# Delta rule outputs split where they are made, and a second merge that loads both operands directly

## The chip, the core and the metric

The kernel runs on one core of one Trainium2 chip. The metric is device time in microseconds (us) of one execution; runs are told by their median. The engines are named as in the profile: PE is TensorE's matmul side, PEld its weight loads, DVE is VectorE, ACT is ScalarE, POOL is GpSimd, and SP is the SyncE queue, which issues nearly all DMAs in order.

## What is computed

One inference step of a decoder layer for two groups of requests that share one set of weights: a prompt of 1024 tokens and a decode group of 8 sequences with 4 tokens each (32 columns). Model width is 1024. Cut to what matters here:

```
h = RMSNorm(x);  p = h @ w_in
  -> attention q|k|v (8 heads x 64), conv input of the delta rule, gate z, decays a, b, gate_A, gate_B
branch A: stick-breaking attention over 8 heads                      -> o_A (512 wide)
branch B: short conv, SiLU, gated delta rule, 4 heads, 128x128 state;
          o = RMSNorm(o) * gdn_norm_w * silu(z)                      -> o_B (4 heads x 128 = 512 wide)
merge:    m = sigmoid(gate_A) * (o_A @ w_pa) + sigmoid(gate_B) * (o_B @ w_pb);  x = x + m @ w_o
mixer:    x = x + relu(RMSNorm(x) @ w_up)^2 @ w_down;  final RMSNorm
```

The change is about o_B on its way from branch B into the product o_B @ w_pb, which is called the second merge here (its steps are named pb).

## The kernel before

Activations are held transposed: 128 features on the partitions, tokens along the row. T = 1056 columns are the 1024 prompt tokens and the 32 decode tokens. Every large product is made of three matmuls with operands split in two. The rounded part is the value in the type fp32r, written by an ACT copy; the rest is the value less the rounded part, written by a DVE subtraction. `dense` multiplies rounded weight by rounded activation, rounded weight by the activation's rest, and the weight's rest by the rounded activation (L137, L138, L139). `load_w` loads a block of weights and splits it in the same way (L127 on ACT, L128 on DVE).

The order of instructions on each engine is not written by hand. The program gives a sequence with priorities, and a planner at build time simulates it and sets the order of each engine's queue; `tc.high_priority()` moves steps ahead, `tc.issue_after` holds a step behind another. Tiles live in pools that are opened and closed like a stack, and a pool that is opened later takes over the space of closed ones. Tiles with one tag share one buffer (or as many as `bufs` says).

The steps in the order of the program, where the change touches them:

1. Four heads of the delta rule, `gdn_head(h)`. Their projections run interleaved with the chunk-wise recurrence (8 chunks of 128 tokens). In a head, `vb` (tag vb, one buffer) is the scaled v, read by the recurrence at L551; `qe` (tag cgb, one buffer) is loaded from cg_d at L489, goes through an exponential on ACT (L490) and a product on DVE (L491), and is read by the recurrence at L568. At the head's end the output is normalised, transposed on PE and multiplied by silu(z) into `zl` (L585). `zl` has the tag cgb too, so it takes qe's buffer, and the next head's qe takes its. L586 stores zl into `o_d[4 + h]` in DRAM.
2. The decode group's delta rule, in one go for all heads and sequences. Its output `dot` goes into the last 32 columns of `o_d[4:8]` (L778). The pools of this part and of the decode attention (`kts` and others) take over the space of the heads' pool.
3. The attention's projections and the prompt's attention, a pipeline over blocks (head, row block): scores on PE (L958, L959), sigmoid on ACT (L960), masking and 1 - s on POOL (L961, L964), a scan on DVE (`pr`, L968) and a product on DVE (L969), transposes on PE (`wt`, L111), and products with v (`po`, L1006). In `pipeline(x0, x1, fill)` other steps are put between the blocks: first the products of the gates (`pd_g`, whose outputs `gt` are stored to gA_d and gB_d, L1073), and from block 34 on the steps of the second merge, `pb_step(j, c, first)`, for 8 blocks of output columns and 4 groups of tokens c (256, 256, 256, 288 columns).
4. The operands of the second merge, `obh[c]` (rounded part) and `obl[c]` (rest), for the four groups of tokens. A group of o_B is loaded from o_d into a staging tile, `ofb0` to `ofb3` (L1111 for the first, L1153 for the others), copied into obh[c] on ACT (L1155), and subtracted into obl[c] on DVE (L1156). ofb0 lies in the pool zp and is loaded ahead of the close of the projections' pools; ofb1 and ofb3 share one buffer of the pool z2p; ofb2 lies in the pool obp beside obh and obl. Between the third and the fourth group two rows of gate B are loaded (`tbs`, L1159); the others are loaded by `pb_step` behind `mark`, the last operand load.
5. `pb_step` multiplies by w_pb with `dense4`, and DVE multiplies the result by gate B into tb (L1174).
6. Then the first merge (o_A @ w_pa, steps pa), w_o, and the mixer.

Of the kernel before, what the change touches and what calls it, by code (L numbers as in the profile page):

```python
# [8 lines left out]
F32 = mybir.dt.float32  # L9
F32R = mybir.dt.float32r  # L10
I32 = mybir.dt.int32
I64 = mybir.dt.int64
AF = mybir.ActivationFunctionType
ALU = mybir.AluOpType
# [4 lines left out]
P = 128  # L19
D = 1024  # L20
NP = 1024
NS = 32
T = NP + NS
# [8 lines left out]
GH = 4  # L32
# [6 lines left out]
def hybrid_step(ctx, tc, x_prompt, x_sample, cache_k, cache_v, page_table, state_conv, state_ssm,  # L39
# [5 lines left out]
    V, S_, G, PE, SY = nc.vector, nc.scalar, nc.gpsimd, nc.tensor, nc.sync  # L45
# [12 lines left out]
    dr = ctx.enter_context(tc.tile_pool(name="dr", bufs=1, space=DRAM))  # L58
# [30 lines left out]
    for t in range(9):  # L89
        xn = sp.tile([P, D], F32, tag="xn", name=f"xn{t}", bufs=7)  # L90
        n = P if t < 8 else NS
# [4 lines left out]
        if t in (1, 3, 5):  # L96
            wp = wpool if t == 1 else gw if t == 5 else sp
            st = wp.tile([P, 8, P], F32, tag="wst", name=f"ws_u0{t}", bufs=1)
# [47 lines left out]
    xT_d, o_d, x1_d = spill("xT_d"), spill("o_d"), spill("x1_d")  # L146
    gA_d, gB_d = spill("gA_d"), spill("gB_d")
    z_d = dr.tile([GH, P, NP], F32, name="z_d")
    q_d = [dr.tile([4, P, NP], F32, name=f"q{x}_d") for x in "hl"]
    k_d = [dr.tile([4, P, NP], F32, name=f"k{x}_d") for x in "hl"]  # L150
    v_d = dr.tile([4, P, NC, P], F32, name="v_d")
# [32 lines left out]
    zp = pool("zp", stack=zctx)  # L184
# [7 lines left out]
    for t in range(9):  # L192
        n = P if t < 8 else NS
# [65 lines left out]
    gk = pool("gk", stack=gctx, side="right")  # L259
# [129 lines left out]
    def gdn_head(h):  # L389
# [12 lines left out]
        for i, (src, tag) in enumerate(((kT, "ms"), (qT, "tv"))):  # L402
            sq = gk.tile([P, NP], F32, tag=tag, name=f"sq{i}{h}")
            S_.activation(sq, src, AF.Square)
            for hf in range(2):
                sqt = gk.tile([P, 512], F32, tag="x2", name=f"sqt{i}{h}{hf}")
                V.transpose(sqt, sq[:, hf * 512:(hf + 1) * 512])
                o = 32 * i + 16 * hf
# [35 lines left out]
        for c0 in range(0, NC, 2):  # L444
            pt = ttile(f"kk{h}_{c0}")
            for c in (c0, c0 + 1):
                sl = slice(c * P, (c + 1) * P)
                o = (c - c0) * 2 * P
                PE.matmul(pt[:, o:o + P], lhsT=kT[:, sl], rhs=kT[:, sl], start=True, stop=True)
                PE.matmul(pt[:, o + P:o + 2 * P], lhsT=kT[:, sl], rhs=qT[:, sl], start=True, stop=True)  # L450
            for c in (c0, c0 + 1):
                sl = slice(c * P, (c + 1) * P)
                o = (c - c0) * 2 * P
# [16 lines left out]
        for k in range(31):  # L470
            nr = 31 - k
            ob = gk.tile([32, 256], F32, tag="ob", name=f"ob{h}_{k}")
# [11 lines left out]
        vb = gk.tile([P, NP], F32, tag="vb", name=f"vb{h}")  # L484
# [50 lines left out]
        for hf in range(2):  # L535
            hs = slice(hf * 512, (hf + 1) * 512)
            p5 = gtile(f"wt{h}_{hf}")
            for i in range(4):
                c = hf * 4 + i
# [7 lines left out]
        st = None  # L547
        for c in range(NC):
# [22 lines left out]
            st = sn  # L571
        SY.dma_start(nss_prompt[0, 0, h], st)
        zl = gk.tile([P, NP], F32, tag="cgb", name=f"zl{h}")
# [9 lines left out]
        for hf, pt in enumerate(tr8(on, f"o{h}", gtile)):  # L583
            sl = slice(hf * 512, hf * 512 + 512)
            V.scalar_tensor_tensor(zl[:, sl], zl[:, sl], gnw, pt, op0=ALU.mult, op1=ALU.mult)  # L585
        SY.dma_start(o_d[4 + h, :, 0:NP], zl)  # L586

    for h in range(GH):
        gdn_head(h)
# [45 lines left out]
    dk = pool("dk", stack=dctx, side="right")  # L635
# [117 lines left out]
    for it in range(3):  # L753
# [3 lines left out]
        mark = V.tensor_tensor(dy, dr_, py[:, 0:P], op=ALU.subtract)  # L757
        if it != 1:
# [16 lines left out]
    dot = dk.tile([P, GH, NS], F32, name="dot")  # L775
    V.scalar_tensor_tensor(dot.rearrange("p h c -> p (h c)"), zs.rearrange("p h c -> p (h c)"), gnw, pot[:, 0:P],
                           op0=ALU.mult, op1=ALU.mult)
    SY.dma_start(o_d[4:8, :, NP:T].rearrange("h p c -> p h c"), dot)  # L778
    dkp = dk.tile([P, P], F32, name="dkp")
    V.tensor_scalar(dkp, knd, degc, None, op0=ALU.mult)  # L780
    vexp = dk.tile([P, NSEQ, P], F32, tag="big", name="vexp")
    mark = V.tensor_tensor(vexp, dy.unsqueeze(1).to_broadcast([P, NSEQ, P]), m84.unsqueeze(2).to_broadcast([P, NSEQ, P]), op=ALU.mult)
# [20 lines left out]
    for p in range(4):  # L803
        for nm, col, keep_s in (("q", 0, qsT), ("k", 512, ksT), ("v", 1024, vsT)):
            hi = lo = f = None
            if nm != "q":
                f = fk.tile([P, T], F32, tag="ft", name=f"{nm}f{p}", bufs=NFT)
# [76 lines left out]
    for g in range(2):  # L884
# [14 lines left out]
        n = 260  # L899
# [207 lines left out]
            if t % 2 == 1 and t >= 3:  # L1107
                fills.append(lambda t=(t - 3) // 2: residual_step(t))
    pipeline(0, SPLIT, fills)
    ofb0 = zp.tile([P, 4, 256], F32, tag="zz", name="ofb0")  # L1110
    SY.dma_start(ofb0, o_d[4:8, :, 0:256].rearrange("k p c -> p k c"))  # L1111
    xctx.close()
    tbctx = ExitStack()
    oa3 = pool("oa3", stack=tbctx)
# [26 lines left out]
    for c in range(len(CX)):  # L1141
        ob_tiles(c)
    for c, (o, n) in enumerate(CX):
        if c == 0:
            st = ofb0
        else:
            if c == 1:
                st = z2p.tile([P, 4, 288], F32, tag="zz", name="ofb1")[:, :, 0:256]
            elif c == 2:
                st = obp.tile([P, 4, 256], F32, name="ofb2")  # L1150
            else:
                st = z2p.tile([P, 4, 288], F32, tag="zz", name="ofb3")
            mark = SY.dma_start(st, o_d[4:8, :, o:o + n].rearrange("k p c -> p k c"))  # L1153
        with tc.high_priority():
            S_.activation(obh[c], st, AF.Copy)  # L1155
            V.tensor_tensor(obl[c], st, obh[c].bitcast(F32), op=ALU.subtract)  # L1156
        if c == 2:
            for j in range(2):
                SY.dma_start(tbs[j], gB_d[j])  # L1159
    wbs = {}  # L1160
# [545 lines left out]
```

## Time and profile before

| | |
|---|---|
| median of 3 runs | 1700.03 us (1699.78 to 1703.91) |
| the profiled execution | time 1701.33 us, span 1699.6 us, mean granted clock 0.995 |
| instructions | 34650 |
| PEld busy | 1616.3 us (95%) |
| DMA | 240.86 MB, mean 142 GB/s |

The profile is of one execution. Its span is counted from the first to the last recorded event, its time is measured around the execution. A busy PE is one whose records overlap without a gap; the granted clock (PEclk) says at what share of full speed it ran.

The span falls into stretches. In the table of windows for 80 to 515 us, in which the four heads run, DVE is busy for 274.23 of 435 us and ACT for 175.45. From 465 us on gate products run beside; the decode group's work lies from about 512 to 616 us, the prompt's attention from 640 to 860 us, the second merge's operands from 745 to 780 us, and its products from 754 to 860 us. The mixer takes most of the rest, 1020 to 1640 us.

In the rows of the timeline the first two columns are start and duration in us; then engine, line, operation, output <- inputs, shape, and in brackets the idle time of the engine before it with what ended it.

### The profile page before, as it was taken

To read this page: it belongs to the slowest core of one execution; us is meant where nothing else is said; L and a number is where in the kernel's file an instruction comes from. 1 tells how busy PE (TensorE), PEld (TensorE's weight loads), DVE (VectorE), ACT (ScalarE), POOL (GpSimd) and SP (SyncE) were. 2 spreads that over 40 slices of the span, in tenths; PEclk is the share of its full clock that TensorE was granted. 3 is DMA by queue.
4 is the path that set the end of the run, shared out by engine and by line. 5 is a ranking of instruction groups with operands and counts; after the bars stand their busy time and mean duration, and the time that the engine had idled before them with its cause. 6 is when DMAs were issued, how large, how long until landed. Compare 5 with 4: busy or idle time off the path is not lost.

```text
span 1699.6 us, 34650 instructions
## 1 busy us (share of the span) xinstructions
PE 1665.5 (98%) x13934; PEld 1616.3 (95%) x13934; DVE 1170.7 (69%) x2335; ACT 778.5 (46%) x1548; POOL 220.7 (13%) x243
## 2 busy tenths in 40 slices
PE   7999999999999999999999999999999999999998
PEld 6999999999999799988999999999999999999998
DVE  6656676877325337789776578877777678688964
ACT  5453434343324225555433455644444564334455
POOL 1110111110004226565300000000000000000000
PEclk9999999999999999999999999999999999999999
DMA  5132233244538577895144545555443765442231
GB/s 182 38 119 81 70 95 104 74 124 129 159 90 240 156 194 180 203 237 178 42 130 144 166 134 159 155 161 162 140 140 117 270 210 190 151 158 97 96 114 78
DMA packets 260205, 240.86 MB, mean 142 GB/s; under 512 B 55906, under 2 KB 217795, under 8 KB 260044
## 3 DMA queue, kind: packets, MB, share of 16 engines
q1 hardware_dynamic: 255094, 227.90, 44.4%
q0 software_dynamic: 3200, 10.52, 2.1%
q8 instruction: 109, 1.79, 0.4%
q10 hardware_dynamic: 1750, 0.23, 0.1%
q14 instruction: 52, 0.43, 0.1%
HBM read 164.02 MB, written 74.58 MB: 140 GB/s over the span
## 4 chain that ended last, share of the span: by engine, by line
PE 89%; DVE 4%; issue 2%; DMA 2%; POOL 1%; ACT 1%; SPq 0%; DVEq 0%; POOLq 0%; ACTq 0%
PE pu L139 6%; PE pu L137 6%; PE pu L138 6%; PE pw L137 6%; PE pw L138 6%; PE pw L139 6%; PE pd_g L137 3%; PE pd_g L138 3%; PE pd_g L139 3%; PE wt L111 1%; PE px L138 1%; PE px L137 1%; PE px L139 1%; PE pd_uk L139 1%; PE po L1006 1%
## 5 line engine op out<-in xcount | busy, mean ns | idle before, releaser
L137 PE MATMUL pu<-Xh,uh 128*128 128x264 f32 x812 | 229.8, 284 | 0.5 <-ACT t L1426 0.5
L139 PE MATMUL pu<-Xh,ul 128*128 128x264 f32 x812 | 230.1, 285 | 0.0
L138 PE MATMUL pu<-Xl,uh 128*128 128x264 f32 x812 | 229.8, 283 | 0.0
L137 PE MATMUL pw<-hc,w 128*128 128x264 f32 x784 | 220.8, 285 | 2.8 <-ACT w L1517 2.4
L138 PE MATMUL pw<-hc,w 128*128 128x264 f32 x784 | 220.0, 286 | 0.0
L139 PE MATMUL pw<-hc,w 128*128 128x264 f32 x784 | 216.3, 286 | 0.0
L137 PEld LDWEIGHTS pu<-Xh,uh 128*128 128x128 f32 x812 | 153.2, 189 | 0.9 <-ACT t L1426 0.7
L138 PEld LDWEIGHTS pu<-Xl,uh 128*128 128x128 f32 x812 | 152.8, 188 | 0.0
L139 PEld LDWEIGHTS pu<-Xh,ul 128*128 128x128 f32 x812 | 152.1, 188 | 0.0
L137 PEld LDWEIGHTS pw<-hc,w 128*128 128x128 f32 x784 | 148.1, 189 | 3.2 <-ACT w L1517 2.6
L137 PE MATMUL pd_g<-xh,wh_g 128*128 128x256 f32 (+1 forms) x512 | 149.9, 293 | 0.0
L138 PE MATMUL pd_g<-xl,wh_g 128*128 128x256 f32 (+1 forms) x512 | 149.6, 292 | 0.0
L139 PE MATMUL pd_g<-xh,wl_g 128*128 128x256 f32 (+1 forms) x512 | 149.0, 291 | 0.0
L138 PEld LDWEIGHTS pw<-hc,w 128*128 128x128 f32 x784 | 147.1, 189 | 0.0
L139 PEld LDWEIGHTS pw<-hc,w 128*128 128x128 f32 x784 | 145.7, 190 | 0.0
L968 DVE TENSOR_TENSOR_SCAN pr<-am 128x127 f32<-128x127 f32 (+7 forms) x64 | 89.5, 1399 | 19.1 <-POOL am L964 15.7
L137 PEld LDWEIGHTS pd_g<-xh,wh_g 128*128 128x128 f32 x512 | 97.2, 190 | 3.2 <-issue 2.6
L138 PEld LDWEIGHTS pd_g<-xl,wh_g 128*128 128x128 f32 x512 | 97.3, 190 | 2.5 <-issue 2.1
L139 PEld LDWEIGHTS pd_g<-xh,wl_g 128*128 128x128 f32 x512 | 97.1, 190 | 2.1 <-issue 2.0
L1517 ACT ACTIVATE w<-a 128x512 fp32r<-128x512 f32 x84 | 46.6, 620 | 94.6 <-PE pw L139 88.2
L1490 ACT ACTIVATE hc<-hc 128x528 fp32r<-128x528 f32 x98 | 62.1, 644 | 28.8 <-DMA hc<-hc_d 26.8
L139 PE MATMUL px<-mh,wl_wo 128*128 128x264 f32 x256 | 72.5, 286 | 1.3 <-DVE wl_wo L1262 1.2
(582 smaller groups left out, 5014.8 us busy)
## 6 DMA issues: line engine op xcount, KB each, us to landing
hc_d<-t SPq DMA_DIRECT2D x27, 924.0 KB
hc<-hc_d SPq DMA_DIRECT2D x94, 264.0 KB
a<-in_w_down_dram SPq DMA_DIRECT2D x52, 256.0 KB
ws_c<-in_w_in_dram SPq DMA_DIRECT2D x16, 512.0 KB
ws_wo<-in_w_o_dram SPq DMA_DIRECT2D x32, 256.0 KB
ua<-in_w_up_dram SPq DMA_DIRECT2D x16, 512.0 KB
ub<-in_w_up_dram SPq DMA_DIRECT2D x16, 512.0 KB
gA_d<-gt SPq DMA_DIRECT2D x8, 528.0 KB
```

The lines of the kernel that those rows point to most:

```text
L111: return PE.transpose(out, in_, ident[:k, :k])
L137: PE.matmul(pt[:, :n], lhsT=wh[k], rhs=xh[k], start=(k == 0), stop=False)
L138: PE.matmul(pt[:, :n], lhsT=wh[k], rhs=xl[k], start=False, stop=False)
L139: PE.matmul(pt[:, :n], lhsT=wl[k], rhs=xh[k], start=False, stop=(k == nk - 1))
L968: V.tensor_tensor_scan(pr[:, n - 1:0:-1], am_r, am_r, 1.0, op0=ALU.mult, op1=ALU.bypass)
L1006: PE.matmul(po[64 * r:64 * r + 64, 0:P], lhsT=vn[:, b, rs], rhs=wts[hh, 2 * m + r][:, b * P:(b + 1) * P], start=(b == 0), stop=(b == 2 * m ...
L1490: S_.activation(tl[:, 0], tl[:, 1].bitcast(F32), AF.Copy)
L1517: S_.activation(tl[:, 0], src, AF.Copy)
```

## The change

Branch B's output is split at its source. At the end of each head, zl is copied on ACT into a new fp32r tile `zh`, which takes the tag vb, and zl less zh is written into zl on DVE. Both are stored, into two new DRAM arrays ob_d[0] and ob_d[1], in place of one store into o_d. The decode group's `dot` is split in the same way (`doh` takes the tag dyt), and two stores take the place of one. In the second merge, obh[c] and obl[c] are loaded directly from the two arrays. The staging tiles ofb0 to ofb3, the four ACT copies and the four DVE subtractions there are gone, and so is the load of ofb0 ahead of the pools' close. `mark` is now the load of the last rest, and the first two rows of gate B follow the first group's loads in the program, not the third's.

```diff
+    ob_d = [dr.tile([GH, P, T], F32, name=f"ob{x}_d") for x in "hl"]
...
             V.scalar_tensor_tensor(zl[:, sl], zl[:, sl], gnw, pt, op0=ALU.mult, op1=ALU.mult)
-        SY.dma_start(o_d[4 + h, :, 0:NP], zl)
+        zh = gk.tile([P, NP], F32R, tag="vb", name=f"zh{h}")
+        S_.activation(zh, zl, AF.Copy)
+        V.tensor_tensor(zl, zl, zh.bitcast(F32), op=ALU.subtract)
+        SY.dma_start(ob_d[0][h, :, 0:NP], zh.bitcast(F32))
+        SY.dma_start(ob_d[1][h, :, 0:NP], zl)
...
-    SY.dma_start(o_d[4:8, :, NP:T].rearrange("h p c -> p h c"), dot)
+    doh = dk.tile([P, GH, NS], F32R, tag="dyt", name="doh", bufs=2)
+    S_.activation(doh, dot, AF.Copy)
+    V.tensor_tensor(dot, dot, doh.bitcast(F32), op=ALU.subtract)
+    for dst, src in zip(ob_d, (doh.bitcast(F32), dot)):
+        SY.dma_start(dst[:, :, NP:T].rearrange("h p c -> p h c"), src)
...
-    ofb0 = zp.tile([P, 4, 256], F32, tag="zz", name="ofb0")
-    SY.dma_start(ofb0, o_d[4:8, :, 0:256].rearrange("k p c -> p k c"))
...
     for c, (o, n) in enumerate(CX):
+        for dst, src in zip((obh[c], obl[c]), ob_d):
+            mark = SY.dma_start(dst.bitcast(F32), src[:, :, o:o + n].rearrange("k p c -> p k c"))
         if c == 0:
-            st = ofb0
-        else:
-            if c == 1:
-                st = z2p.tile([P, 4, 288], F32, tag="zz", name="ofb1")[:, :, 0:256]
-            elif c == 2:
-                st = obp.tile([P, 4, 256], F32, name="ofb2")
-            else:
-                st = z2p.tile([P, 4, 288], F32, tag="zz", name="ofb3")
-            mark = SY.dma_start(st, o_d[4:8, :, o:o + n].rearrange("k p c -> p k c"))
-        with tc.high_priority():
-            S_.activation(obh[c], st, AF.Copy)
-            V.tensor_tensor(obl[c], st, obh[c].bitcast(F32), op=ALU.subtract)
-        if c == 2:
             for j in range(2):
                 SY.dma_start(tbs[j], gB_d[j])
```

## The prediction

> **What bounds the kernel now.** I read the page's busy shares and chain first, then the stretch that the change touches most, in windows.
>
> ```profile
> span 1699.6 us, 34650 instructions
> PE 1665.5 (98%) x13934; PEld 1616.3 (95%) x13934; DVE 1170.7 (69%) x2335; ACT 778.5 (46%) x1548; POOL 220.7 (13%) x243
> PE 89%; DVE 4%; issue 2%; DMA 2%; POOL 1%; ACT 1%; SPq 0%; DVEq 0%; POOLq 0%; ACTq 0%
> ```
>
> TensorE is the bound: 1665.5 of 1699.6 us busy and 89% of the chain. Time can only be won where PE stands idle or runs at a lowered clock, 34 us in all, and much of that is start and end. So I looked for PE's idle time around the three places of the change: the ends of the four delta-rule heads (257 to 512 us), the decode group's output (569 us) and the second merge's operands (745 to 793 us). The next fence is a table of windows: length, then busy time of PE, PEld, DVE, ACT and POOL, the granted clock, DMA share and GB/s.
>
> ```profile
> core 0: us, PE busy (x) PEld busy (x) DVE busy (x) ACT busy (x) POOL busy (x), PEclk, DMA share, GB/s
> 745.00:754.00 9.00, 8.98 (x82) 7.18 (x81) 5.55 (x6) 7.55 (x17) 4.52 (x5) 1.00 0.74 244
> 754.00:758.06 4.06, 1.79 (x15) 1.03 (x11) 4.05 (x3) 2.93 (x8) 3.97 (x3) 1.00 1.09 379
> 758.06:763.00 4.94, 4.94 (x25) 4.56 (x26) 4.94 (x5) 1.26 (x3) 4.78 (x5) 0.65 1.08 244
> 763.00:768.00 5.00, 5.00 (x52) 4.42 (x50) 4.76 (x7) 3.66 (x9) 2.98 (x5) 1.00 1.02 243
> 768.00:774.00 6.00, 5.92 (x57) 4.92 (x56) 5.39 (x7) 4.55 (x10) 3.10 (x4) 1.00 1.05 416
> 774.00:779.00 5.00, 4.38 (x29) 3.65 (x30) 4.90 (x4) 1.53 (x4) 1.99 (x2) 1.00 0.45 122
> 779.00:784.00 5.00, 4.20 (x32) 3.64 (x31) 4.90 (x6) 1.86 (x3) 3.07 (x2) 1.00 0.83 231
> 784.00:788.00 4.00, 4.00 (x31) 3.25 (x29) 4.00 (x5) 1.66 (x4) 2.04 (x2) 1.00 1.05 210
> 788.00:793.00 5.00, 5.00 (x40) 4.23 (x37) 4.90 (x4) 2.46 (x5) 0.52 (x2) 1.00 0.05 8
> ...
> 800.00:860.00 60.00, 60.00 (x538) 54.93 (x537) 40.53 (x60) 26.63 (x58) 18.05 (x26) 1.00 0.13 38
> ```
>
> The reader is to see three things. From 754 on VectorE is full (4.05 of 4.06, 4.94 of 4.94, 4.90 of 5.00). PE is idle in just those rows: 2.27 us before 758.06, then 0.08, 0.62 and 0.80, with the 0.02 of the first row 3.79 us. And in the row 758.06 to 763.00 PE counts as busy all the time at a clock of 0.65, which costs 0.35 x 4.94 = 1.73 us. From 800 on PE is full again, so what is won before 793 is kept. **The ceiling of this stage is 3.79 + 1.73 = 5.5 us.**
>
> Who holds VectorE there is in the timeline, with what PE waits for behind its brackets:
>
> ```profile
> 756.02 1.99 DVE L1156 TENSOR_TENSOR obl<-ofb,obh 128x1024 fp32r<-128x1024 f32 x1
> 759.02 1.30 DVE L1156 TENSOR_TENSOR obl<-ofb,obh 128x1024 fp32r<-128x1024 f32 x1
> 766.59 1.63 DVE L1156 TENSOR_TENSOR obl<-ofb,obh 128x1024 fp32r<-128x1024 f32 x1
> 775.45 2.09 DVE L1156 TENSOR_TENSOR obl<-ofb,obh 128x1152 fp32r<-128x1152 f32 x1
> ...
> 758.06 0.38 PE L138 MATMUL pb<-obl,wh_pb 128*128 128x256 f32 x1 [2.11 <-DVE obl L1156]
> 759.11 0.42 PE L139 MATMUL pb<-obh,wl_pb 128*128 128x256 f32 x1
> ...
> 777.59 0.40 PE L138 MATMUL pb<-obl,wh_pb 128*128 128x288 f32 x1 [0.62 <-DVE obl L1156]
> ```
>
> The four subtractions take 1.99 + 1.30 + 1.63 + 2.09 = 7.0 us, amid the scans (pr) and products (s) of the attention, and the largest PE wait (2.11) and the 0.62 wait both end with one of them.
>
> **Part 1, removed: four ACT copies and four DVE subtractions of the merge.** VectorE had 43.4 us of work in 745 to 793 (the column's sum); without 7.0 it has 36.4 in 48, so it no longer paces this stage: PE's work there, 44.2 busy us less 1.73 of lowered clock, is 42.5. The copies on ACT (rows below) take 4.3 us from an engine that is never full there. I take the waits after 763 as gone: 0.08 + 0.62 + 0.80 = **-1.5 us**. Next late after them is PE itself. Ends: 0, if other attention steps hold PE just there, and -1.5.
>
> **Part 2, moved: the operands come by DMA alone.** Now ofb0 is fetched long ahead into a buffer of its own, and the others in turn. These rows give the times of issue and the sizes.
>
> ```profile
> 648.29 0.39 SPq L1111 DMA_DIRECT2D ofb<-o_d  x1
> ...
> 747.13 0.38 SPq L1073 DMA_DIRECT2D gB_d<-gt  x1
> ...
> 753.50 0.38 SPq L1153 DMA_DIRECT2D ofb<-o_d  x1
> ...
> vn<-v_d SPq DMA_DIRECT2D x4, 512.0 KB
> ofb<-o_d SPq DMA_DIRECT2D x3, 512.0 KB
> ...
> kh<-kh_d SPq DMA_DIRECT2D x16, 256.0 KB
> ```
>
> After the change no part is ahead: obh0 and obl0 lie in the pool that takes over the space of the projections' operands and of the gate buffers, the last of which is stored at 747.13. The only load into that pool today is ofb2, at 753.50, so I put the first new loads there in SP's order. Two of 512 KB are 1.05 MB: at 379 GB/s 2.8 us, at 244 GB/s 4.3 us, so 756.3 to 757.8 if nothing is in front. In front of them can be a vn and two head loads, 1.0 MB or as much again: 759.1 to 762.1. The first operands are thus there between 756.3 and 762.1 against 758.06 now; I take the middle, 759.2, as the DMA share is 1.0 and above from 754 to 774. That would be +1.1 us of wait. Against it, the scores' products, queued behind these subtractions on VectorE, come up to 2.0 us earlier and give PE attention work for the gap; half of the wait of 2.27 filled that way is -1.1, and with the gap's new length (3.4) half is -0.6 net. Of the lowered clock I count nothing as won. So **-0.6 us**; ends: -2.27 - 1.73 = -4.0 (no wait, no lowered clock) and 762.1 - 758.06 = +4.0. Later operands are ahead of need: each further pair is 2.8 to 4.3 us, so pair 4 by 779 at the very latest and by about 768 at 379 GB/s, where today its subtraction ends at 777.5. The burst puts 8 x 512 KB where 3 x 512 stood (2.7 MB, 7 to 11 us of queue); behind it on SP are the next head's q and k and the gate rows, which are first needed after 779.
>
> The clock: after an idle of 2.11 us PE's products take 0.42 instead of 0.28 us from 758.9 on. The Trainium skill, TensorE: Matmul & The Clock Gate, section "Part 1: The HAM clock gate", says that the array falls to half rate after an idle window of about 3.4 us and recovers after as much sustained work. The drop agrees, the length of idle before it (2.11 us) is shorter than that window; by it a wait cut to half would cost no clock at all and the sum below would be 1.7 us lower. By the row a short wait is enough, so I leave the 1.73 us in.
>
> **Part 3, added: the split in each head and two stores for one.** Per head an ACT copy and a DVE subtraction of 128x1024, four times; the store of 512 KB becomes two.
>
> ```profile
> L1155 ACT ACTIVATE obh<-ofb x4: 1048/1064/1163, 753.0 to 770.9; 128x1024 fp32r<-128x1024 f32 x3, 128x1152 fp32r<-128x1152 f32 x1
> 434.22 1.23 DVE L836 TENSOR_TENSOR kf<-kf,kh 128x1024 f32<-128x1024 f32 x1 [0.42 <-PE t_nk L111]
> 257.09 0.32 SPq L586 DMA_DIRECT2D o_d<-zl  x1
> 259.72 0.32 SPq L489 DMA_DIRECT2D cgb<-cg_d  x1
> ...
> 263.39 1.28 ACT L490 ACT_TABLE_LOAD   x1 [2.77 <-DMA cgb<-cg_d]
> ...
> 283.60 0.39 PE L551 MATMUL y<-vb,U 128*128 128x128 f32 x2
> ...
> 293.99 0.39 PE L568 MATMUL o<-st,cgb 128*128 128x128 f32 x2
> ...
> 80.00:515.00 435.00, 431.25 (x3822) 424.92 (x3821) 274.23 (x702) 175.45 (x411) 44.36 (x41) 1.00 0.35 106
> ```
>
> 4 x 1.06 us on ACT and 4 x 1.23 on VectorE, at 40% and 63% busy in that stretch, while PE has 431.25 of 435: the work itself hides. What gets longer is a chain of buffers. zl shares its buffer with the next head's qe (tag cgb), and qe's load waits for zl's store (issued 257.09, the load 259.72, so 2.6 us). With copy, subtraction and a second store that is 1.06 + 1.23 + some 1 us = 3.3 us later, three times. ACT already stands 2.77 us before qe's exponential, and what is behind it there (the weights' copies) would stand longer. And zh takes the buffer of vb, so the next head's vb, now written before zl is made, has to wait for zh's store, to about 262. Both are needed late: vb at 283.60, qe at 293.99, some 20 us of slack. Price on PE: from 0 to 3 x 3.3 = +10 us, nearest to the 3.75 us that PE idles in this whole stretch of 435. I take **+0.5**. Below nothing is excluded, since the steps only add work before a store, except by a luckier order.
>
> **Part 4, the decode group and the handover.** Two instructions on 128x128 and one more small store, then the last head's store later by the same 3.3 us.
>
> ```profile
> 516.28 0.17 DVE L892 COPY kts<-ksT 128x16 f32<-128x16 f32 x1 [0.25 <-DMA o_d<-zl]
> ...
> 510.00:522.00 12.00, 12.00 (x101) 11.92 (x101) 10.71 (x44) 1.62 (x4) 2.72 (x3) 1.00 1.06 301
> ```
>
> A small copy stands for the store of zl, and the gather's indices stand behind it on VectorE; PE has gate products throughout (12.00 of 12.00). I take 0; if that cover went, +3.3. Below nothing: no reason.
>
> **The sum**: -1.5 - 0.6 + 0.5 + 0 = -1.6 us. The profiled execution has a span of 1699.6 us and a time of 1701.33; the median of the three runs is 1700.03. I put the difference to the median: **1698.4 us**. A measurement here can tell some 0.3%, 5.1 us, from no change.
>
> **The rivals.**
>
> Full relief: PE's wait before 758 closes because the order lets attention run there, the clock stays up, and VectorE's slack lets PE run dense: -5.5 and no price in the heads, 1694.5. For it: VectorE is full in every row where PE idles. Against it: the first operands now depend on the busiest queue of the kernel. Chance 0.21, two thirds of it below 1694.9, as the new order may close gaps elsewhere.
>
> Late operands: the burst lands at the late end, PE stands from 756 to 762 before the first merge products, at half clock after it: +4.0 - 1.5 + 0.5 = +3.0, 1703.0. For it: a DMA share of 1.0 to 1.09 from 754 to 774. Against it: 416 GB/s in one of these rows. Chance 0.17.
>
> Slower, from the heads: ACT's order puts weight copies behind qe's exponential, and PE runs out of other products three times for 3.3 us: +9.9 - 2.1 = +7.8, 1707.8. It decides if more than two of the three handovers reach PE (6.6 - 2.1 is 4.5). For it: ACT waits 2.77 us there now. Against it: 20 us of slack, and an order made anew that can put these copies first. Chance 0.12.
>
> The change does nothing: waits move from the subtractions to the next link (scans, POOL), 1700. Chance 0.10.
>
> **How the numbers follow.** My own case, -0.5 to -4.5 us, has the remaining 0.40, and its time is the prediction; a first wait cut to half with no lowered clock after it, -1.6 - 1.7 = -3.3, 1696.7, is 0.10 of this 0.40. (That is the outcome by the section of the Trainium skill's page TensorE: Matmul & The Clock Gate cited above.) Faster by over 0.3%: 0.14 from full relief and 0.05 from an own case that falls lower, 0.19. Slower: 0.12 from the heads and 0.03 of late operands, 0.15. Within: 0.66. The range goes down to the full relief with some luck of order, 1693, and up past late operands, 1704.5.
>
> **What would show it.** Right: no instruction of the merge's split, VectorE at most 37 us busy in the 48 us from the last gate product on, no PE wait of over 0.3 us for a pair after the first, and two stores per head with no new PE wait before 515. Wrong: PE waits for a DMA of obl at the first pair for over 3.5 us; ACT waits of over 4 us before L490 with PE waiting for a weight's rest; or PE's busy share falling in stretches that the change does not touch, because the whole order is computed anew.

## The result, and the profile after

The change makes the kernel slower: 1713.53 us median of 5 runs (1709.87 to 1719.91) against 1701.92 us (1699.78 to 1703.91), a ratio of 1.0071 [1.0051, 1.0091], +12.1 us [8.7, 15.5]. The prediction was 1698.4 us. The profiled run is the longest of the five, 1719.91 us, so its losses are some 6 us above those of a median run.

The page of the changed kernel, its span, busy times and chain of waits:

```profile
span 1717.0 us, 34697 instructions
PE 1671.8 (97%) x13934; PEld 1622.0 (94%) x13934; DVE 1169.8 (68%) x2336; ACT 779.8 (45%) x1549; POOL 223.3 (13%) x243
PE 83%; DMA 5%; DVE 5%; issue 3%; ACT 2%; POOL 1%; SPq 0%; DVEq 0%; POOLq 0%; ACTq 0%
```

PE's share of the chain fell from 89% to 83%, DMA's rose from 2% to 5%. VectorE's busy time hardly moved (1170.7 to 1169.8): the split was moved, not removed.

To see where the time went I cut the span into windows of 5 us and summed, for each stage, length less PE's busy time times the granted clock. This is the time lost on PE, idle and slow clock together:

| kernel | ratio to before [95%] | us | heads 80-515 | handover 515-710 | merge 710-860 |
|---|---|---|---|---|---|
| before | 1 | | 3.9 | 1.7 | 5.4 |
| changed | 1.0071 [1.0051, 1.0091] | +12.1 | 8.8 | 7.4 | 10.6 |
| e1 heads alone | 1.0022 [1.0005, 1.0039] | +3.7 | 9.1 | 4.4 | 5.5 |
| e2 merge alone | 1.0040 [1.0022, 1.0058] | +6.8 | 3.8 | 1.7 | 11.1 |
| e3 changed, zl apart | 1.0168 [1.0141, 1.0195] | +28.6 | 17.3 | 5.3 | 13.1 |
| e4 before, zl apart | 1.0033 [1.0016, 1.0050] | +5.6 | 10.7 | 0.7 | 5.5 |
| e5 changed, qe freed | 1.0118 [1.0098, 1.0137] | +20.2 | 12.1 | 8.3 | 12.8 |
| e6 before, qe freed | 1.0037 [1.0022, 1.0052] | +6.3 | 8.2 | 11.2 | 5.5 |
| e7 merge, no rests | 1.0004 [0.9993, 1.0016] | +0.7 | 5.0 | 4.7 | 11.5 |
| e8 merge, first ahead | 1.0004 [0.9993, 1.0015] | +0.7 | 4.0 | 5.2 | 3.5 |
| e9 work only | 1.0028 [1.0013, 1.0043] | +4.8 | 6.0 | 3.9 | 5.7 |
| e10 vb's buffer only | 1.0060 [1.0038, 1.0082] | +10.2 | 11.4 | 5.5 | 5.6 |
| e11 store later only | 1.0089 [1.0069, 1.0109] | +15.1 | 14.4 | 4.5 | 5.5 |
| e12 second store only | 1.0015 [1.0000, 1.0029] | +2.6 | 5.8 | 3.3 | 5.3 |
| e13 changed, chain first | 1.0104 [1.0077, 1.0131] | +17.7 | 11.5 | 3.6 | 10.2 |
| e14 before, chain first | 1.0097 [1.0071, 1.0124] | +16.5 | 16.3 | 9.8 | 5.4 |
| e15 last head and decode | 1.0004 [0.9988, 1.0020] | +0.7 | 4.2 | 2.8 | 5.7 |
| e16 before, first split early | 1.0006 [0.9991, 1.0021] | +1.0 | 3.8 | 6.1 | 3.9 |
| e17 changed, first ahead | 1.0019 [1.0003, 1.0035] | +3.2 | 6.0 | 10.0 | 2.6 |
| e18 changed, vb free | 1.0098 [1.0073, 1.0122] | +16.8 | 10.5 | 6.4 | 9.2 |

The us column is the ratio times the median of the kernel before in the same set of runs. In the six sets (changed; e1-e4; e5-e8; e9-e12; e13-e16; e17-e18) the kernel before took 1701.9, 1702.0, 1709.0, 1701.1, 1702.2 and 1710.4 us, so times of different sets are not compared, only ratios. The stage columns are of one profile each. Kernels with the heads' code of the kernel before (before, e2, e7, e8, e16) lose 3.8 to 5.0 us in the heads, and those with the changed heads (changed, e1, e17) 6.0 to 9.1, so a difference of 1 to 3 us between two profiles says little. In e5 to e8 and in e17 and e18 the handover column holds 2.2 to 4.9 us of waits that end with nothing but PE's own issue, and no other run has such waits there.

Before to changed the three stages lose 4.9, 5.7 and 5.2 us more, 15.8 of the span's 17.4.

**The merge.** Windows of the changed kernel (length; busy PE, PEld, DVE, ACT, POOL; granted clock, DMA share, GB/s):

```profile
core 0: us, PE busy (x) PEld busy (x) DVE busy (x) ACT busy (x) POOL busy (x), PEclk, DMA share, GB/s
758.00:763.00 5.00, 5.00 (x52) 4.05 (x50) 4.63 (x5) 4.44 (x11) 1.19 (x2) 1.00 0.79 186
763.00:767.00 4.00, 3.98 (x35) 3.09 (x31) 3.90 (x4) 3.62 (x10) 3.91 (x4) 1.00 0.86 276
767.00:772.00 5.00, 2.76 (x16) 1.79 (x15) 4.69 (x4) 2.44 (x6) 4.91 (x4) 1.00 1.02 296
772.00:777.00 5.00, 5.00 (x40) 4.46 (x39) 4.59 (x5) 2.43 (x6) 5.00 (x6) 0.66 1.09 272
...
790.00:795.00 5.00, 2.83 (x18) 2.59 (x17) 4.90 (x4) 0.00 (x0) 1.67 (x1) 0.86 1.02 233
795.00:800.00 5.00, 3.56 (x17) 3.26 (x16) 2.21 (x5) 0.00 (x0) 0.00 (x0) 0.50 1.06 395
```

and rows of its SP queue and of PE there, the last gate product, three waits and the first product of the merge:

```profile
763.67 0.38 SPq L123 DMA_DIRECT2D ws_pb<-in_w_pb_dram  x1
...
767.73 0.59 SPq L1152 DMA_DIRECT2D obh<-obh_d  x1
...
771.65 3.80 SPq L1152 DMA_DIRECT2D obh<-obh_d  x1
```

```profile
757.94 0.29 PE L139 MATMUL pd_g<-xh,wl_g 128*128 128x288 f32 x1
771.78 0.95 PE L111 MATMUL wt<-ident,s 128*128 128x128 f32 x7 [2.12 <-DVE s L978]
777.42 0.28 PE L137 MATMUL pb<-obh,wh_pb 128*128 128x256 f32 x1
792.99 0.39 PE L137 MATMUL pb<-obh,wh_pb 128*128 128x256 f32 x1 [2.17 <-DVE tb L1170]
796.88 0.58 PE L137 MATMUL pb<-obh,wh_pb 128*128 128x256 f32 x1 [1.44 <-DVE tb L1170]
```

From the last gate product to the first merge product it is 19.5 us (757.94 to 777.42); in the kernel before it was 9.2 (745.34 to 754.53). In these 19.5 us PE has only the attention, and DVE paces the attention with its scans and products (4.69 of 5 us busy, the 2.12 us wait for `s`). It is not the lack of a merge operand that PE shows as its wait, it is the lack of other work. And the larger half of the loss comes behind the first product: from 788 on PE waits 0.31, 2.17 and 1.44 us for `tb`, VectorE's product with gate B, which has its place behind the widest scans. With the clock of 0.86 and 0.50 the ten us from 790 lose 5.8 of the stage's 10.6.

**The heads.** The handover to the last head in windows, before and then changed:

```profile
430.00:440.00 10.00, 9.02 (x125) 8.35 (x124) 4.49 (x7) 5.14 (x9) 0.00 (x0) 1.00 0.74 238
440.00:450.00 10.00, 10.00 (x99) 9.40 (x99) 2.92 (x6) 2.83 (x7) 0.00 (x0) 1.00 0.65 185
```

```profile
430.00:440.00 10.00, 7.56 (x82) 7.03 (x81) 6.57 (x9) 5.15 (x10) 0.00 (x0) 0.93 0.41 144
440.00:450.00 10.00, 10.00 (x110) 9.48 (x109) 2.39 (x5) 2.12 (x5) 0.00 (x0) 0.90 0.98 262
```

and its rows in the timeline, the first step of the inverse's loop and the transposition that makes U, before and then changed, there with the PE step that waits for U:

```profile
386.98 0.20 DVE L474 TENSOR_TENSOR ob<-ms,tv 32x31 f32<-32x31 f32 x1 [0.83 <-DMA ms<-ms_d]
425.95 1.25 DVE L494 STREAM_TRANSPOSE U<-t 128x1024 f32<-128x1024 f32 x1 [1.75 <-DMA t<-tv_d]
```

```profile
396.46 0.20 DVE L475 TENSOR_TENSOR ob<-ms,tv 32x31 f32<-32x31 f32 x1 [3.65 <-DMA ms<-ms_d]
434.93 1.25 DVE L495 STREAM_TRANSPOSE U<-t 128x1024 f32<-128x1024 f32 x1 [2.15 <-DMA t<-tv_d]
...
436.32 0.69 PE L504 MATMUL l<-U,E 32*32 32x32 f32 x32 [1.64 <-DVE U L495]
```

The last head's inverse starts 9.5 us later and U is 9.0 us later. PE waits for it, and in 430 to 450 its clock is down as well.

**The handover to decode group and attention.** Before, PE was busy in all of 610 to 660. In the changed kernel the load of a gate weight is issued at 647.76 instead of 635.89, behind the attention's first loads. ACT stands 7.82 us for it, and the sigmoid behind its copy (`s`, L969) is what PE waits for. The window, and the rows of SP, ACT and PE:

```profile
655.00:660.00 5.00, 1.77 (x15) 1.57 (x14) 3.31 (x3) 1.93 (x4) 0.00 (x0) 1.00 0.36 72
```

```profile
647.76 0.38 SPq L237 DMA_DIRECT2D ws_c<-in_w_in_dram  x1
658.07 1.06 ACT L127 ACTIVATE wh_g<-ws_c 128x1024 fp32r<-128x1024 f32 x1 [7.82 <-DMA ws_c<-in_w_in_dram]
660.05 0.50 PE L967 MATMUL sc<-kh,qs 128*128 128x512 f32 x1 [3.28 <-ACT s L969]
```

### The profile page after: what moved, and what is told of

It is laid out like the page before. It is cut to its first block, busy times and chain, and to the rows that moved or that the text cites. A ratio compares the mean times of both kernels' runs of the same rounds, so it can differ in the third digit from the quotient of the medians.

```text
span 1717.0 us, 34697 instructions
## 1 busy us (share of the span) xinstructions
PE 1671.8 (97%) x13934; PEld 1622.0 (94%) x13934; DVE 1169.8 (68%) x2336; ACT 779.8 (45%) x1549; POOL 223.3 (13%) x243
## 4 chain that ended last, share of the span: by engine, by line
PE 83%; DMA 5%; DVE 5%; issue 3%; ACT 2%; POOL 1%; SPq 0%; DVEq 0%; POOLq 0%; ACTq 0%
PE pu L139 6%; PE pu L137 6%; PE pu L138 6%; PE pw L139 5%; PE pw L138 5%; PE pw L137 5%; PE pd_g L137 3%; PE pd_g L138 3%; PE pd_g L139 3%; PE wt L111 1%; PE po L1015 1%; PE px L139 1%; PE px L138 1%; PE px L137 1%; PE pd_z L137 1%
## 5 line engine op out<-in xcount | busy, mean ns | idle before, releaser
L977 DVE TENSOR_TENSOR_SCAN pr<-am 128x127 f32<-128x127 f32 (+7 forms) x64 | 90.3, 1411 | 10.2 <-POOL am L973 6.3
L973 POOL TENSOR_SCALAR am<-s 128x128 f32<-128x128 f32 (+7 forms) x64 | 78.2, 1222 | 8.2 <-DVE pr L977 3.0
```

The source lines that it names most:

```text
L973: G.tensor_scalar(am[:, :n], s[:, :n], -1.0, 1.0, op0=ALU.mult, op1=ALU.add)
L977: V.tensor_tensor_scan(pr[:, n - 1:0:-1], am_r, am_r, 1.0, op0=ALU.mult, op1=ALU.bypass)
```

## The experiments

My first theory was of three losses with a place each: in the heads, the chain from the store of zl to qe's load, exponential and product, which holds the conv buffer that the next head's v takes; at the handover, the last head's later store; in the merge, the doubled loads.

### e1 and e2: each half alone

e1 keeps the split in heads and decode group and stages the merge as before; e2 keeps the heads and loads both operands directly.

```diff
e1 (against changed)   - direct loads   + staging, copy, subtraction as before, from ob_d[0]
e2 (against before)    - staging, copy, subtraction
                       + obh[c], obl[c] loaded directly, both from o_d[4:8]
```

> The split in the heads and in the decode group stays, with its two stores each; the merge is as before (staging tiles, ACT copies, DVE subtractions) and takes its staging from the array of rounded parts, so the rests are left out of the second merge. Theory (three separate losses): the longer chain zl store -> qe load -> exponential -> product, which holds a conv buffer of the next head, costs 5 us by the end of the fourth head, and the later last store another 4 to 6 us by the first po product (640); the merge is as before, so 1710 to 1713 us, and the last gate product comes 9 to 12 us later than in the kernel before. Rival 1 (the merge's doubled loads are the whole loss): within 2 us of the kernel before. Rival 2 (luck of an order made anew by every edit): a loss that does not sit at the handovers between heads.

> Heads and decode group as before, with one store of the unsplit output; the merge loads both operands directly, both from that one array, so the split is left out. Theory: from the last gate product to the end of the pb products it loses some 4 us as the changed kernel did (17.0 less 12.6 us of drift), 1704 to 1707 us; up to the first po product (640) it stands within 1 us of the kernel before. Rival 1 (merge is the whole loss): 1711 to 1714 us. The prediction's own sum for this part alone: -2.1 us, 1699 to 1700 us.

e1 costs +3.7 us [0.9, 6.6], e2 +6.8 [3.7, 9.9]: the halves add to 10.5, inside the interval of the whole. e1 came below its range and e2 at the upper end of it. The stages show the same: e1 loses in the heads what the changed kernel does (9.1 and 8.8) and in the merge what the kernel before does (5.5), e2 the other way round (3.8 and 11.1). So the merge's loss needs no edit of the heads. e2's PE and SP rows show the same gap, 20.7 us from the last gate product (746.02) to the first pb:

```profile
757.71 0.59 SPq L1143 DMA_DIRECT2D obh<-o_d  x1
```

```profile
761.23 0.97 PE L111 MATMUL wt<-ident,s 128*128 128x128 f32 x7 [2.12 <-DVE s L969]
766.76 0.28 PE L137 MATMUL pb<-obh,wh_pb 128*128 128x256 f32 x1
```

### e7, e8, e16 and e17: what the merge loses by

```diff
e7 (against e2)       - loads of obl[c]   + obl[c] = obh[c]
e8 (against e2)       + ob0h = zp.tile(..., tag="zz"); ob0l = pre.tile([P, 3, 256])   # loaded where ofb0 was
                      + ob0x = obp.tile([P, 1, 256])                                  # fourth block of the rest
e16 (against before)  + ofb0 split as soon as it is loaded, the rest in place, 3 of 4 rounded blocks into pre
e17 (against changed) + as e8
```

> The merge alone (heads as before), without the four loads of rests: the rounded operand stands in for the rest, so the rests are left out. Half the bytes, no split. Theory A (the loss of the merge is bandwidth: 8 loads of 512 KB in front of gate rows and heads): most of the 6.8 us go, 1700 to 1703 us. Theory B (the loss is the first pair's lateness, some 10 us after the gates' last product instead of being fetched ahead): first pb still some 17 us after that product, 1705 to 1708 us.

> The merge alone (heads as before, both operands from the one array, so the split is left out), with the first group's operands fetched ahead as the first staging tile was (the rounded part into its buffer, three of four blocks of the rest into a space beside the attention's tiles, the fourth block in the burst). Theory B (lateness of the first pair): first pb back to within 11 us of the last gate product, 1699 to 1703 us. Theory A (bandwidth): 7 loads of 512 KB are still issued in the same stretch, 1705 to 1709 us.

> The kernel before, with heads, stores and loads unchanged; only the first group's operands are split early, as soon as its staging tile is there (650 on): the rest in place, the rounded part of three of the four blocks in a space beside the attention's tiles, the fourth block as before. DVE's 1.99 us subtraction at 756 and the 2.11 us wait with the clock's drop behind it should go: lost time of the merge 2 to 4 us (5.4 before), ratio 0.998 to 1.000. Rival (the DVE work moves to 650 to 710, where DVE is 40 of 50 us busy and paces the attention): 1.000 to 1.002.

> The changed kernel, heads and decode group untouched, with the first group's operands fetched ahead of the pools' close (the rounded part into the old staging tile's buffer, three of the four blocks of the rest beside the attention's tiles). Theory (two losses that add): first pb within 5 us of the last gate product (19.5 in the changed kernel), lost time of the merge 3 to 5 us instead of 10.6, heads as in the changed kernel (8.8); ratio to the kernel before 1.002 to 1.005. Rival (the loss in the heads comes out as before, the merge only shifts): 1.006 to 1.008.

Both e7 and e8 take +0.7 us [-1.2, 2.7 and -1.2, 2.6] against e2's +6.8, so in time both remedies take the merge's loss away. e8 is the clearer, as six of the eight loads and a small one (`ob0x`, 128 KB) still come in one burst there: the gap is 3.2 us and the stage loses 3.5. e7's order put the first load in front (issued at 754.93, 2.6 us after the last gate product at 752.33), the gap is 7.6 us, but its profile still loses 11.5 us in the stage and 3.7 of it is a wait for that load:

```profile
759.92 0.58 PE L137 MATMUL pb<-obh,wh_pb 128*128 128x256 f32 x1 [3.72 <-DMA obh<-o_d]
```

There is no profile of the kernel before on that chip to set this against, so e7, whose time is in the range of theory A, does not part bandwidth from lateness. e17 does the fix on the whole change, with the heads' code untouched: the gap is 3.2 us again, the merge loses 2.6, and the ratio falls from 1.0071 to 1.0019 [1.0003, 1.0035], at the low end of what was expected. The merge's loss is thus the lateness of the first pair: with it ahead, PE's waits for `tb` shrink to one of 1.45 us (e8) and 1.62 (e17). Fetching it ahead is worth some 9 us to the changed kernel, and the +3.2 us that are left are close to what e1 costs. e16 shows what the idea is worth to the kernel before: the stage loses 3.9 instead of 5.4, but the time is the same (+1.0 [-1.5, 3.6]). That is the rival's time, though not its mechanism: it is ACT that stands 5.67 us for the load of `ofb` ahead of the early copy (654.96), and a copy of `wt` behind it holds PE. From the waits of e16's PE, 605 to 665:

```profile
PE wt L111 <- ACT wt L981: 3.1, 1, 3.1
```

### e3 and e4: zl in another buffer

```diff
-        zl = gk.tile([P, NP], F32, tag="cgb", name=f"zl{h}")
+        zl = gk.tile([P, NP], F32, tag="U", name=f"zl{h}")
```

> The changed kernel, with zl in the buffer of U (dead from the last chunk's y product on, written again some 75 us later) and not in that of qe, so that the next head's qe is loaded without waiting for the stores. Theory: the product qe comes before the conv of the next head's v again, the third handover loses nothing, and the 5 us by the end of the fourth head go away or turn into a gain: 1706 to 1709 us. Rival (the loss in the heads is the added work of ACT and DVE, or the vb buffer that zh takes): no change against the changed kernel, 1712 to 1715 us.

> The kernel before, with zl in the buffer of U. Theory (the store of zl holds back qe, and qe's product a conv buffer): it does so in the kernel before too, by the 2.6 us from store to load and the wait for the table load; without it the stretch from 250 to 515 us, in which PE idles 2.5 us and more, wins 1 to 3 us: 1698 to 1701 us. Rival (only the added 3 to 6 us reach PE, before that there is slack): within 0.5 us of the kernel before.

Both are slower, e3 by 28.6 us. The premise was wrong: heads overlap, and U of the next head is written ahead of the end of this one (245.01 in the kernel before, where zl is stored at 257.09). With zl there the next U came at 266.28 (e3) and 258.84 (e4). These two tell nothing of qe; they show what a late U costs.

### e5 and e6: qe's buffer freed at the product

```diff
-            V.scalar_tensor_tensor(zl[:, sl], zl[:, sl], gnw, pt, op0=ALU.mult, op1=ALU.mult)
+            V.scalar_tensor_tensor(on[:, sl], zl[:, sl], gnw, pt, op0=ALU.mult, op1=ALU.mult)
```

and copy, rest and stores from `on` (e5) or the one store from `on` (e6).

> The changed kernel with the same copy, subtraction and stores, but the gated output is written into the normalised output's own buffer (nw, which the next head writes again only some 25 us later, 255.5 to 280.2) and the rest is made there; so the buffer of qe is free as soon as the product has been read, and neither subtraction nor store stands ahead of the next qe's load. zh stays in the buffer of vb. Theory (store chain -> qe -> conv buffer costs the heads 5 us): PE loses at most 3.2 us between 250 and 515 instead of 8.4 (idle and clock together), and the median is 1706 to 1709 us. Rival 1 (added work, or vb made late): the stretch loses as before this edit, 1712 to 1715 us.

> The kernel before, with the gated output written into the buffer of the normalised output and stored from there, so that qe's load waits for the product alone, not for the store (2.5 us sooner, three times). Theory: in the kernel before the chain was just not late; PE idles 3.1 us from 250 to 515, of which 0 to 2 us can go: 1699.5 to 1702 us. Rival (chain already costs there): 1696 to 1699 us.

The theory of one chain falls here. There are three handovers between the four heads, at about 257, 345 and 431 us, and the conv of the last head's v follows the second. In e5 the exponential of this second handover is at 354.78, close to the 353.02 of the kernel before (362.49 in the changed kernel), and the heads still lose 12.1 us. The ACT row and then three DVE rows of e5:

```profile
354.78 1.06 ACT L491 ACTIVATE cgb<-cgb 128x1024 f32<-128x1024 f32 x1 [0.93 <-DMA cgb<-cg_d]
```

```profile
359.03 1.29 DVE L487 TENSOR_TENSOR vb<-t_v,s 128x512 f32<-128x512 f32 x2
372.53 0.71 DVE L408 STREAM_TRANSPOSE sqt<-sq 128x512 f32<-128x512 f32 x1
396.79 0.19 DVE L475 TENSOR_TENSOR ob<-ms,tv 32x31 f32<-32x31 f32 x1 [2.96 <-DMA ms<-ms_d]
```

The loop starts at 396.79, as late as without the remedy. Other work now stands ahead of the norms: vb at 359.03 (337.68 before), the last norm transposition at 372.53 (367.76 before). And e6, which takes a wait away from the kernel before and holds the normalised output's buffer until the store, is 6.3 us slower. Profiles of the same chip with unedited heads (e7, e8) lose 5.0 and 4.0 in that stage, e5 and e6 12.1 and 8.2.

### e9 to e12 and e18: one burden of the heads at a time

```diff
e9   + zh = on.bitcast(F32R); copy zl -> zh; on = zl - zh; then the old store of zl     # results unused
e10  + zh in tag vb; copy zl -> zh; then the old store of zl                            # result unused
e11  + zh = on.bitcast(F32R); copy zl -> zh; zl = zl - zh; then the one store of zl
e12  + SY.dma_start(o2_d[h, :, 0:NP], zl)                                               # behind the old store
e18  (against changed) zh = on.bitcast(F32R) in place of a tile of tag vb
```

> The kernel before with the copy and the subtraction added in each head (4 of each), both written into the normalised output's own buffer, which nothing needs for 25 us; their results are not used, the unsplit zl is stored once as before. Only the work is added: no store, no buffer that the next head waits for. Theory (buffers, not work): within 1.5 us of the kernel before. Rival (the added 1.06 us of ACT and 1.23 us of DVE at a full handover is the price): +3 to +5 us, with PE idle of 6 us or more between 250 and 515 (3.1 in the kernel before).

> The kernel before with the ACT copy alone, into the buffer of vb, as zh does in the changed kernel; the result is not used, there is no subtraction, and one store of zl as before. It takes vb's buffer from the next head until the copy is through and so moves vb (0.6 us of DVE twice) from ahead of the handover (246.2, 337.7) into it. If the loss of the heads is vb's place: +2 to +5 us. If it is the chain from store to qe: within 1.5 us. If it is any new order: +3 to +5 us here too, with another pattern of waits.

> The kernel before with copy and subtraction ahead of its one store (the copy into the normalised output's buffer, the rest in place of zl, and only the rest is stored, so the rounded part is left out of the second merge). vb is undisturbed; store and qe's load come 2.3 to 4 us later, as in the changed kernel, less the second store. If the chain from store to qe is the price: +2 to +4 us, with PE waiting for U near 433. If it is vb's place: within 1.5 us.

> The kernel before with zl stored twice, into two arrays: no copy, no subtraction, vb undisturbed; qe's load waits for two stores instead of one, some 0.5 to 1 us later. By the chain from store to qe: 0 to +1.5 us. By vb's place or the added work: 0. By any new order: +3 us or more.

> The changed kernel with zh in the normalised output's buffer, so that vb is written at its old time; copy, subtraction and both stores as in the change, merge as in the change. If vb's place is what the heads lose by: lost time from 80 to 515 at 4 to 6 us (8.8), ratio 1.004 to 1.006. If it is the order computed anew (a kernel with only the store later lost 14.4 there with vb undisturbed): 9 to 14 us, ratio 1.008 to 1.012.

In lost time of the heads, over the 3.9 of the kernel before: the work alone 2.1, a second store alone 1.9, vb's buffer 7.5, the store later 10.5. The last holds the work too, so together these would be some 20; the change, which holds all four, costs 4.9. The times say the same: e9 +4.8 us (the range of its rival), e12 +2.6 (between two expectations), e10 +10.2 and e11 +15.1 (above all of them), but e1, with all four, +3.7. So the parts do not add, and no single one is shown to be the price. Nor is vb's place: with vb free the changed kernel gets worse (e18, 1.0098, in the range given to a new order). Each edit has the planner compute another order. That the order decides is the reading that is left, argued and not shown.

e12 shows how little is enough. It adds four stores and nothing else, yet the second handover's exponential comes at 361.96 instead of 353.02. SP rows of before, then of e12:

```profile
345.22 0.34 SPq L586 DMA_DIRECT2D o_d<-zl  x1
347.85 0.34 SPq L489 DMA_DIRECT2D cgb<-cg_d  x1
349.68 0.38 SPq L123 DMA_DIRECT2D ws_av<-in_w_in_dram  x1
...
351.22 2.08 SPq L833 DMA_DIRECT2D v_d<-ntv  x1
```

```profile
349.56 0.43 SPq L588 DMA_DIRECT2D o_d<-zl  x1
351.51 0.38 SPq L123 DMA_DIRECT2D ws_av<-in_w_in_dram  x1
352.09 0.62 SPq L833 DMA_DIRECT2D out_dram<-ntv  x1
352.76 2.22 SPq L835 DMA_DIRECT2D v_d<-ntv  x1
355.30 0.33 SPq L490 DMA_DIRECT2D cgb<-cg_d  x1
```

Before, qe's load went out ahead of the next weight and of the stores of v; now it stands behind them, 5.7 us after the store instead of 2.6. The changed kernel has the same sequence (its last store of zl at 350.66, qe's load at 354.93). In e12 the loop then starts at 396.56 and PE waits for U:

```profile
435.94 0.69 PE L504 MATMUL l<-U,E 32*32 32x32 f32 x32 [1.85 <-DVE U L495]
```

### e13 to e15

```diff
e13 (changed), e14 (before)  + with tc.high_priority():   # around the norms, rk, s, E1, E2 and kk of a head
e15 (against e1)             + heads 0 to 2 store zl once, unsplit
```

> The changed kernel with one edit: the steps of a head from the squares of k and q to the decay products of the inverse (norms, rk, s, E1, E2, kk) are given high priority in the order. Theory (the chain from the conv to the inverse's loop and U has no slack at the handover, and the new order lets other DVE work in front): the last head's loop starts before 393 (396.5 in the changed kernel, 387.0 before), the time lost on PE from 80 to 515 falls from 8.8 to under 6 us, 2 to 4 us faster than the changed kernel, ratio to the kernel before 1.004 to 1.006. Rival (luck of the order): lost time in the heads 6 to 14 us as in the other edits, ratio 1.007 or more.

> The kernel before with the same priority for that chain. Theory (chain without slack): lost time in the heads at or below 3.9 us, ratio 0.998 to 1.001. Rival (the order of the kernel before is a lucky one, any new one costs): heads lose 6 us or more, ratio 1.002 or more.

> Only the last head and the decode group split and store twice; heads 0 to 2 store once as before; the merge is as before and takes the array of rounded parts (the rests of the last head and the decode group are left out). The heads' stage must be as in the kernel before (lost time 3.9 us). If the last head's later store alone makes the handover lose: 515 to 710 loses 3 to 5 us (1.7 before), ratio 1.001 to 1.003. If that loss is a sequel of the earlier one: under 2.5 us there, ratio 0.999 to 1.001.

Priority for the chain to the inverse did not help. The last loop starts at 398.80 (e13) and 400.88 (e14), later than in either kernel, and e14 is 16.5 us slower than the same program without it. Both ratios are in the rival's range. So going first does not cure this chain, and the rival, that the order of the kernel before is one that other orders rarely match, stands.

e15 has the last head and the decode group split. Its heads lose 4.2, as they should, its handover 2.8, between the two expectations, and its time is +0.7 us [-2.0, 3.4]. So the last head's own later store is worth about 1 us in the profile. That the rest of the changed kernel's 7.4 is a sequel of the heads ending late fits this, but no run shows it by itself.

## Why the prediction was wrong

The sum said -1.6 us and the runs say +12.1. The terms of the merge had the wrong sign, the heads' term was too small, and the handover's was put at nothing.

**Part 2 (-0.6; the merge alone, parts 1 and 2, measured +6.8 instead of -2.1).** The step that failed first is the arrival of the first operands. My additions put it 11.0 to 16.8 us after the gates, and the first product came after 19.5. "I put the first new loads there in SP's order" (753.50, 8.2 us after the last gate product) is the smaller error: they were issued 9.8 us after it in the changed kernel and 11.7 in e2. SP issues in order, and the load stands behind a weight load that waits 3.5 us for its buffer (ws_pb at 763.67), a v, stores and heads. From issue to first product it was another 9.7 and 9.0 us, where I had priced 2.8 to 4.3 us, and 8.6 at the latest, by the bytes alone.

The second failed step is "the scores' products ... give PE attention work for the gap". They did not, because the scans themselves pace the attention. The 19.5 us to the first merge product and the 48 us from the last gate product, in windows of the changed kernel:

```profile
757.94:777.42 19.48, 17.22 (x138) 13.79 (x136) 18.18 (x16) 13.35 (x31) 15.47 (x14) 0.91 0.95 258
757.94:805.94 48.00, 41.82 (x310) 35.48 (x309) 38.48 (x37) 21.89 (x48) 27.91 (x25) 0.89 1.01 280
```

Over the 48 us DVE was busy 38.48, close to the "at most 37" that I had named as the sign of being right, and yet PE lost 6.2 us of idle and more by a clock of 0.89. The mean hides the stretch that counts: in the first 19.5 us DVE was busy 18.18. Even without the subtractions the attention's scans and products filled it there, and PE had nothing else to do: the gate products had ended and the merge had not begun.

**Part 1 (-1.5).** The step that failed is "it no longer paces this stage", with PE itself as the next late. The waits for `obl` are gone, but in the changed kernel PE waits 3.92 us for `tb` on VectorE from 788 to 797, where the kernel before waited 0.80 (782.91). With the first pair ahead the stage loses 3.5 (e8) or 2.6 (e17) where the kernel before loses 5.4. That is a gain of 2 to 3 us, but it comes from the first wait (2.11) and the clock behind it; later waits are still there, for `tb` 1.45 and 1.62. And e8 as a whole is not faster than the kernel before.

**Part 3 (+0.5; measured +3.7 for heads and decode group).** "Both are needed late ... some 20 us of slack" is the step that failed. I measured slack to the recurrence. The first reader that matters is nearer: the product that makes qe holds a conv buffer, and the conv of the next head's v starts right behind it (product 354.11 and conv 355.71 before, 363.58 and 365.78 after). Of the 3.3 us per handover, the exponentials came 4.4, 9.5 and 11.3 us later (264.69, 353.02 and 439.44 before, 269.10, 362.49 and 450.71 after), and in the second qe's load had also lost its place in SP's queue. "The work itself hides" does not hold either: e9, the work alone, took +4.8 us [2.2, 7.3]. But the chain to qe is not the whole answer: e5 removed it at the second handover and lost more. What the runs support is a weaker statement: the handover between heads had no slack to give in this order, and each of the edits tried on all four heads lost 2 to 13 us there, e6's removal of a wait among them. Which link carries the changed kernel's 4.9 us stays open.

**Part 4 (0; the stage lost 5.7 more).** The cover was gone, as the other end of that part allowed, but by another way than the last store: PE waited 3.28 us for a sigmoid behind a gate weight's copy on ACT, and a clock of 0.66 followed. e15, with the last head and the decode group split, loses 1.1 more than the kernel before, so most of it is not the last store's own.

**The clock.** The first wait of 2.11 us was followed by a clock of 0.65 before; in the changed kernel one of 2.12 us is followed by 0.66 in 772 to 777. In e1 the same wait is followed by a full clock, as its PE row and window show:

```profile
768.00:773.00 5.00, 5.00 (x48) 4.61 (x48) 5.00 (x5) 2.46 (x5) 4.92 (x5) 1.00 1.10 244
```

```profile
767.09 0.39 PE L138 MATMUL pb<-obl,wh_pb 128*128 128x256 f32 x1 [2.11 <-DVE obl L1165]
```

Of shorter ones, 1.64 us at 436.32 in the changed kernel was followed by 5 us at 0.73, and 1.67 at 777.32 in e1 by 5 us at 1.00. So the 1.73 us that I left in is not a fixed price of such a wait. The Trainium skill, TensorE: Matmul & The Clock Gate, section "Part 1: The HAM clock gate", says that the activity window runs freely, and that for this reason the slow stretch at a kernel's start differs from run to run. The traces fit that sentence, with one outcome at 0.65 and one at 1.00; by its window of 3.4 us none of these waits should have lowered the clock, and of the three long ones two did.

**The rivals.** Late operands (+3.0) and slower from the heads (+7.8) came both at once, which I had not priced. The mechanism I gave for the heads, weight copies of ACT behind qe's exponential, is not what the traces show: ACT's waits ahead of it at the three handovers are 2.60, 1.59 and 1.06 us after the change, none near the 4 us that I had named. Nor did PE wait for a DMA of obl. Of the signs of being wrong the last one came, PE's busy share falling where nothing is edited, at 655 to 660. The range ended at 1704.5 because I took the two as alternatives.

No version here beats the kernel before. The best of the full change is e17 at 1.0019.

## What to carry to other kernels

When a load replaces a copy, ask what the consuming engine does until it lands, and look at that stretch alone: a mean over the whole stage hides it. Put the first group's load ahead of the pool that it waits for; here that took the gap from 19.5 to 3.2 us with six of the eight loads still in the burst. Slack of a buffer is measured to its first reader and to what that reader holds, not to the last use. Where a planner orders every engine anew, the cost of a small edit in a stage without slack can't be added up from its parts. So try the edit of one stage at a time and keep those that cost nothing.

## What the runs showed of the hardware

The kernel before took 1702.0, 1709.0, 1701.1, 1702.2 and 1710.4 us (medians of 29, 26, 23, 23 and 17 runs, in the sets of e1 to e18 in their order) on different chips, a spread of 0.5% that is larger than most effects here. On the two chips with the longer times (e5 to e8, e17 and e18) PE shows waits ended by nothing but its own issue, up to 1.0 us each and 2.2 to 4.9 us in all from 515 to 710; on the others there are none. They do not make up the whole difference of some 8 us. From the waits of e8:

```profile
PE dks L745 <- issue: 1.9, 4, 1.0
```
